# RWKV time mixing on one core: a store moved behind each crossbar transpose, three loads issued one unit later

## The chip, the core and the metric

The kernel runs on one core of a Trainium2 chip. The metric is the device time of one execution in microseconds (us), lower being better; before the change three runs have a median of 201.7 us (201.13 to 202.95). The core has a matrix engine (TensorE, "PE" in the profile, with its weight loads as "PEld"), a vector engine (DVE), a scalar engine (ACT), a general engine (POOL, also GpSimd), and a sync engine (SP) that here only issues transfers. Transfers run on 16 DMA engines that all issuers share.

## What is computed

For x of 16 batches by 2048 positions by 256 channels, in float32:

```python
x_prev[:, 1:, :] = x[:, :-1, :]           # zero at the first position
xv = x * time_mix_v + x_prev * (1 - time_mix_v)
xr = x * time_mix_r + x_prev * (1 - time_mix_r)
v = xv.reshape(-1, d_model) @ value_weight
r = xr.reshape(-1, d_model) @ receptance_weight
r_sigmoid = 1.0 / (1.0 + np.exp(-r))
out = (r_sigmoid * v).reshape(-1, d_model) @ output_weight
```

The key branch of the reference does not reach the output, and the kernel does not compute it.

## The kernel before

The work is cut into 64 **units** of 512 positions, four to a batch; unit g belongs to batch g // 4. For every unit TensorE makes the receptance product (into `psum_r`), ACT its sigmoid (`s_sb`, L591), TensorE the value product (`psum_v`), DVE the product of both (`z_sb`, L639), and, one or two units later, TensorE the output product (`psum_o`), which ACT copies into an output tile (L405). The mixing with the shifted input is made on DVE, POOL and ACT (`mix`: a scaled copy, L306, L316 or L571, and an addition, L328). POOL does one scaled copy per unit, after the additions that DVE makes for that unit.

All of it needs x with channels on the partitions. There are two ways to that:

- Batches 0 to 9 are loaded into SBUF as bf16, transposed by TensorE (`ps_t`, L250) and copied out by ACT (L267).
- Batches 10 to 15 are loaded and cast by POOL's DMA queue into a DRAM tile (`x_both`, L148, or in two halves, L144, for batches 12 and 15), and a **crossbar transpose** issued from SP (L231, `by_dma`) brings three batches at a time into SBUF (`xt_both`). The first, for batches 10 to 12, is issued in unit 27, the second, for 13 to 15, in unit 39 (`T_AT`). Each waits for the landing of all its loads.

The order on every engine is the order of the program; nothing is rescheduled. So SP issues stores and transposes one after another, and one that waits holds up all behind it. POOL's scaled copies and the loads that POOL issues stand in one queue as well.

The outputs of two units, a pair, share one tile of 1 MB (`o_sb`, or in the later part four tiles of the `x_bf` pool) and go out with one store when the second unit of the pair has been copied. What is done with the store of a pair is decided in `output` by the number of that second unit, g:

```python
            if g in FIRST:
                firsts.setdefault(FIRST[g], []).append(pair)
            elif g in WAITING:
                kept.setdefault(WAITING[g], []).append(pair)
            else:
                store(nc.sync, *pair)
```

A store under `FIRST` is issued in the unit given there, in front of the transpose, after the first half of the last load of the group has landed (`after=half`). A store under `WAITING` is issued in that unit, behind the transpose. All others are issued at once. `STAGE_AT` names the units in which POOL issues the loads of batches 13, 14 and 15, at the end of the unit, behind POOL's scaled copy; each of these loads also waits for the landing of the first crossbar transpose (`last_t`).

Of the kernel before, what the change touches and what calls it, by code (L numbers as in the profile page):

```python
# [15 lines left out]
def kernel(  # L16
# [42 lines left out]
    FREE = CROSS  # L59
    LATE_O = CROSS - 2  # L60
    T_AT = {27: 10, 39: 13}
    FIRST = {25: 27, 29: 39}
    WAITING = {31: 39, 33: 39, 35: 39}
    STAGE_AT = {34: 13, 35: 14, 36: 15}
    GROUPS = [(2, 3), (4, 5, 6), (7, 8, 9), (10, 11, 12), (13, 14, 15)]
    HALVED = (12, 15)
    SPARE = 9 * UB // 2
# [60 lines left out]
    def load(b):  # L128
        if b >= STAGED:
            group = next(q for q in GROUPS if b in q)  # L130
            if b == group[0]:
                x_both[b] = dpool.tile([len(group), P, J, D], BF16, name="x_both")
            x_bf[b] = x_both[group[0]][b - group[0]]
        else:
            x_bf[b] = xpool.tile([P, J, D], BF16, name="x_bf")
        if b < BYUNIT:
            for e in range(UB):
                nc.gpsimd.dma_start(
                    out=x_bf[b][:, e * UJ : (e + 1) * UJ, :], in_=unit_rows(x, b, e)[:, 0]
                )  # L140
            return
        if b in HALVED:
            return [
                nc.gpsimd.dma_start(out=x_bf[b][:, j : j + J // 2], in_=rows(b)[:, j : j + J // 2])  # L144
                for j in (0, J // 2)
            ]
        run = 8192 if b < LONG else 16384
        return nc.gpsimd.dma_start(out=x_bf[b], in_=rows(b), max_dma_last_dim=run)  # L148
# [165 lines left out]
    def scale_pool(piece, after):  # L314
        b, m, _, _ = piece
        op = nc.gpsimd.tensor_scalar(  # L316
            out=mixed(piece)[:, :, 1],
            in0=xt[b][:, slots(piece), 1],
            scalar1=c_sb[:, m, 1:2],
            scalar2=1.0,  # L320
            op0=ALU.mult,
            op1=ALU.mult,
        )
        tc.add_manual_dep(op.ins, after.ins.name, SYNC, reason="one at a time")
# [67 lines left out]
    def output(g, z):  # L392
# [20 lines left out]
        elif e % 2 == 1:  # L413
            pair = (b, (e - 1) * UJ, (e + 1) * UJ)
# [5 lines that stand above are left out]
# [159 lines left out]
    for g in range(NU - 1):  # L579
# [65 lines left out]
        for p in pooled[g]:  # L645
            wrap_slots(p, after=last)
            scale_pool(p, last)
        if g in STAGE_AT:
            b = STAGE_AT[g]
            loads[b] = load(b)  # L650
# [40 lines left out]
```

## Time and profile before

| | |
|---|---|
| median of three runs | 201.7 us |
| profiled execution: time, span | 202.56 us, 200.8 us |
| granted TensorE clock | 0.997 |
| 1 MB stores from `o_sb`, from `x_bf` | 24 and 4 |
| first crossbar transpose: issued, landed | 104.50 us, 120.23 us |
| loads of batches 13, 14, 15 issued | 120.76, 122.44, 124.16 and 124.72 us |
| second crossbar transpose issued | 139.90 us |
| last store issued, landed | 196.38 us, 199.62 us |

Instruction times in the profile are counted from the start of the span. A busy share is an average over the whole run; the share of the DMA engines in a stage says whether transfers queue there, and the time from the issue of a transfer to its landing says how long that queue is. A wait is put down to the event that came last before it ended as far as the semaphores tell; where the engine named had been done long before, the real releaser was another, often a DMA. In the same way the time in which SP writes out a transpose (13.69 and 13.03 us) is listed as if it were a wait. The window sums give, for a stretch of the span, each engine's busy time with the number of instructions, then the granted clock, the share of the DMA engines' time, and what they moved. That share can read somewhat over 1 in the transposes, where packets overlap.

Sigmoids of ACT (L591) mark the units: unit 27 begins at 93.75 us, unit 34 at 114.17, unit 35 at 117.05, unit 36 at 119.42, unit 39 at 128.08, unit 50 at 157.87 and unit 62 at 190.17.

### The profile page before, as it was taken

What the parts mean: (1) busy time and instruction counts of PE and PEld (TensorE: products, weight loads), DVE (VectorE), ACT (ScalarE), POOL (GpSimd) and SP (SyncE); (2) the same over time, 40 slices, a digit from 0 to 9 for tenths busy, and PEclk for the clock granted to TensorE, in tenths of its full rate; (3) what the DMA queues carried; (4) which work ended last, traced back from release to release, by engine and by line L of the source; (5) the groups of instructions that cost most, each with busy time, mean ns of one, the idle gap of its engine ahead of it and who ended that gap; (6) DMA issues with size and microseconds to landing.
All of it is one profiled execution on the core that took longest, in us unless ns stands there. A gap on an engine that the chain in (4) does not pass through costs nothing.

```text
span 200.8 us, 3819 instructions
## 1 busy us (share of the span) xinstructions
PE 192.8 (96%) x1389; PEld 122.7 (61%) x1389; DVE 184.6 (92%) x289; ACT 179.2 (89%) x209; POOL 84.1 (42%) x115
## 2 busy tenths in 40 slices
PE   8999999999999999999999999899999899999990
PEld 7556676666666666666666665466666456666670
DVE  0999999999999999899999997999999999999970
ACT  3699899999999999999999999889999899999980
POOL 1765543363542446342442329444444434444200
PEclk9999999999999999999999999999999999999998
DMA  5999999999999999999988999999999999999994
GB/s 177 219 186 217 222 282 273 277 283 273 295 308 292 297 274 286 286 281 309 313 339 175 212 324 237 212 207 297 180 239 330 418 433 423 418 415 416 402 361 176
DMA packets 36555, 58.05 MB, mean 289 GB/s; under 512 B 25781, under 2 KB 27065, under 8 KB 32697
## 3 DMA queue, kind: packets, MB, share of 16 engines
q1 hardware_dynamic: 32176, 41.29, 59.6%
q0 software_dynamic: 4208, 16.39, 41.3%
q8 instruction: 11, 0.18, 0.3%
q10 hardware_dynamic: 152, 0.13, 0.2%
q14 instruction: 8, 0.06, 0.1%
HBM read 34.34 MB, written 39.85 MB: 369 GB/s over the span
## 4 chain that ended last, share of the span: by engine, by line
PE 67%; DMA 21%; ACT 4%; POOL 3%; issue 2%; DVE 1%; SPq 0%; POOLq 0%; DVEq 0%
PE psum_v L336 20%; PE psum_o L360 19%; PE psum_r L336 18%; DMA xt_both<-x_both 16%; PE ps_t L250 7%; DMA x_bf<-in_x_dram 2%; DMA w_f<-n_receptance_weight_dram 2%; POOL mix L316 2%; ACT xt_both L267 1%; PE ps_t L360 1%; ACT o_sb L405 1%; ACT s_sb L591 1%; DVE z_sb L639 1%; ACT mix L571 1%; POOL x_both L148 1%
## 5 line engine op out<-in xcount | busy, mean ns | idle before, releaser
L316 POOL TENSOR_SCALAR mix<-xt_both,c_sb 128x1024 bf16<-128x1024 bf16 (+1 forms) x55 | 61.3, 1114 | 87.2 <-DVE mix L328 83.8
L328 DVE TENSOR_TENSOR mix<-mix,xt_both 128x1024 bf16<-128x1024 bf16 x112 | 77.5, 702 | 2.4 <-POOL mix L316 1.0
L639 DVE TENSOR_TENSOR z_sb<-s_sb,psum_v 128x1024 bf16<-128x1024 bf16 (+1 forms) x64 | 76.7, 1200 | 3.0 <-PE psum_v L336 1.3
L336 PEld LDWEIGHTS <-w_bf 128*128 128x128 bf16 x516 | 48.8, 98 | 40.4 <-issue 1.2
L591 ACT ACTIVATE s_sb<-psum_r 128x1024 bf16<-128x1024 f32 x63 | 65.1, 1034 | 5.2 <-PE psum_r L336 4.9
L336 PE MATMUL psum_v<-mix,w_bf 128*128 128x512 bf16 (+1 forms) x256 | 65.3, 377 | 0.9 <-DVE z_sb L639 0.8
L336 PE MATMUL psum_r<-mix,w_bf 128*128 128x512 bf16 (+1 forms) x252 | 64.3, 377 | 0.0
L360 PE MATMUL psum_o<-wo_bf,z_sb 128*128 128x256 bf16 x486 | 63.2, 272 | 0.7 <-ACT o_sb L405 0.7
L360 PEld LDWEIGHTS <-z_sb 128*128 128x128 bf16 x512 | 49.7, 98 | 20.6 <-issue 2.0
L405 ACT COPY o_sb<-psum_o 128x1024 f32<-128x1024 f32 x50 | 51.1, 1022 | 5.1 <-PE psum_o L360 5.1
L267 ACT COPY xt_both<-ps_t 128x1024 bf16<-128x1024 bf16 x32 | 32.8, 1034 | 0.0
L250 PEld LDWEIGHTS <-x_bf 128*128 128x128 bf16 x304 | 19.6, 98 | 9.0 <-DMA x_bf<-in_x_dram 1.9
L250 PE MATMUL ps_t<-ident,x_bf 128*128 128x128 bf16 x304 | 22.7, 219 | 0.2
L306 DVE TENSOR_SCALAR mix<-xt_both,c_sb 128x1024 bf16<-128x1024 bf16 (+1 forms) x47 | 21.1, 458 | 0.0
L571 ACT ACTIVATE mix<-xt_both,c_sb 128x1024 bf16<-128x1024 bf16 x14 | 16.2, 1158 | 0.0
L328 DVE TENSOR_TENSOR mix<-mix,xt_first 128x1024 bf16<-128x1024 bf16 x15 | 10.7, 717 | 0.1
L405 ACT COPY x_bf<-psum_o 128x1024 f32<-128x1024 f32 x10 | 10.1, 1014 | 0.0
L306 DVE TENSOR_SCALAR mix<-xt_first,c_sb 128x512 bf16<-128x512 bf16 x22 | 6.5, 348 | 0.3 <-ACT xt_first L260 0.2
L267 ACT COPY xt_first<-ps_t 128x1024 bf16<-128x1024 bf16 x6 | 6.2, 1026 | 0.0
L148 POOL DMA_DIRECT2D x_bf<-in_x_dram x8 | 5.7, 714 | 0.0
L491 POOL COPY xt_first<-xt_first 128x254 bf16<-128x254 bf16 x5 | 2.0, 395 | 6.6 <-DVE mix L328 6.6
L316 POOL TENSOR_SCALAR mix<-xt_first,c_sb 128x512 bf16<-128x512 bf16 x6 | 4.1, 689 | 0.7 <-DVE mix L328 0.2
(70 smaller groups left out, 55.6 us busy)
## 6 DMA issues: line engine op xcount, KB each, us to landing
out_dram<-o_sb SPq DMA_DIRECT2D x24, 1024.0 KB, 15.0
x_bf<-in_x_dram POOLq DMA_DIRECT2D x8, 1024.0 KB, 21.1
x_both<-in_x_dram POOLq DMA_DIRECT2D x4, 1024.0 KB, 13.8
out_dram<-x_bf SPq DMA_DIRECT2D x4, 1024.0 KB, 12.4
x_both<-in_x_dram POOLq DMA_DIRECT2D x4, 512.0 KB, 17.8
x_bf<-in_x_dram POOLq DMA_DIRECT2D x6, 256.0 KB, 6.2
out_dram<-x_bf SPq DMA_DIRECT2D x6, 256.0 KB, 4.4
o_sb<-in_x_dram SPq DMA_DIRECT2D x4, 256.0 KB, 3.8
```

Source lines behind the costliest of these rows:

```text
L148: return nc.gpsimd.dma_start(out=x_bf[b], in_=rows(b), max_dma_last_dim=run)
L250: nc.tensor.transpose(out=ps[:, jj], in_=src[:, jj, ko * P : (ko + 1) * P], identity=idn)
L267: nc.scalar.copy(out=xt[b][:, j0 : j0 + UJ], in_=ps)
L306: nc.vector.tensor_scalar(out=mixed(piece)[:, :, ko], in0=xt[b][:, slots(piece), ko], scalar1=c_sb[:, m, ko : ko + 1], scalar2=None, op0=A ...
L316: op = nc.gpsimd.tensor_scalar(out=mixed(piece)[:, :, 1], in0=xt[b][:, slots(piece), 1], scalar1=c_sb[:, m, 1:2], scalar2=1.0, op0=ALU.mul ...
L328: return nc.vector.tensor_tensor(out=mixed(piece), in0=mixed(piece), in1=xt[b][:, slots(piece, 1)], op=ALU.add)
L336: nc.tensor.matmul(out=ps[:, mo, :], lhsT=w_bf[:, m, ko, mo * P : (mo + 1) * P], rhs=mixed((b, m, e * TU + lo, e * TU + hi))[:, :, ko], st ...
L360: nc.tensor.matmul(out=ps[:, slot, :], lhsT=z[:, ko, jj * P : (jj + 1) * P], rhs=wo_bf[:, ko, :], start=(ko == 0), stop=(ko == KO - 1),)
L405: nc.scalar.copy(out=o[:, j0 : j0 + UJ, :], in_=ps)
L571: nc.scalar.activation(out=mixed(piece)[:, :, ko], in_=xt[b][:, slots(piece), ko], func=ACT.Copy, scale=c_sb[:, m, ko : ko + 1],)
L591: nc.scalar.activation(out=s_sb, in_=ps_r, func=ACT.Sigmoid)
L639: nc.vector.tensor_tensor(out=z_sb[:, :, c : c + n], in0=s_sb[:, :, c : c + n], in1=ps_v[:, :, c : c + n], op=ALU.mult,)
```

## The change

Three tables of unit numbers are altered, nothing else:

```diff
     T_AT = {27: 10, 39: 13}
-    FIRST = {25: 27, 29: 39}
-    WAITING = {31: 39, 33: 39, 35: 39}
-    STAGE_AT = {34: 13, 35: 14, 36: 15}
+    FIRST = {23: 27, 27: 39}
+    WAITING = {25: 27, 29: 39, 31: 39, 33: 39, 35: 39}
+    STAGE_AT = {35: 13, 36: 14, 37: 15}
```

The stores keep their order among each other. On SP's queue both transposes move one place ahead:

```text
before: ... 21  23  25*  [10-12]  27  29*  [13-15]  31  33  35  37 ...
after:  ... 21  23*  [10-12]  25  27*  [13-15]  29  31  33  35  37 ...
        numbers: second unit of the pair stored; * waits for a half load; [ ] crossbar transpose
```

The store of units 22 and 23, issued at once before, now waits for the first half of batch 12; the store of units 24 and 25 goes behind the first transpose; the store of units 26 and 27 takes the place between the halves of batch 15; the store of units 28 and 29 goes behind the second transpose. On POOL's queue the loads of 13, 14 and 15 each move behind one more scaled copy. The instructions of PE, DVE and ACT and their order are the same.

## The prediction

> A difference under 1% (about 2 us) can hardly be told from none here: the three runs before lie between 201.13 and 202.95 us. "Store 23" below is the 1 MB store of the pair of units 22 and 23, named by its second unit; T10 and T13 are the two crossbar transposes, named by their first batch.
>
> **What bounds the kernel now.** I read first the page's busy shares and slices.
>
> ```profile
> PE 192.8 (96%) x1389; PEld 122.7 (61%) x1389; DVE 184.6 (92%) x289; ACT 179.2 (89%) x209; POOL 84.1 (42%) x115
> ...
> DMA  5999999999999999999988999999999999999994
> GB/s 177 219 186 217 222 282 273 277 283 273 295 308 292 297 274 286 286 281 309 313 339 175 212 324 237 212 207 297 180 239 330 418 433 423 418 415 416 402 361 176
> ```
>
> TensorE is nearly full, but so are the DMA engines, and the last eight slices run at 400 to 430 GB/s: stores alone, at their peak. So two things can set the end. Next, the chain of waits round the two transposes:
>
> ```profile
> 104.50 15.73 DMA xt_both<-x_both
> 120.27 0.47 issue
> 120.76 0.57 POOL x_both L148
> 121.36 1.13 POOL mix L316
> 122.49 0.50 POOL x_both L148
> 123.02 1.18 POOL mix L316
> 124.20 0.81 POOL x_both L144 x2
> 125.27 1.14 POOL mix L316
> 126.43 1.17 ACT mix L571
> ...
> 139.90 16.64 DMA xt_both<-x_both
> 156.77 1.01 ACT o_sb L405
> ```
>
> T10 lands at 120.2; only then may POOL issue the load of batch 13, and POOL's multiplications queue behind it. T13 starts when the last half of batch 15 has landed (139.8), and the chain runs through it to ACT. The waits of 114 to 131 us give what the first costs:
>
> ```profile
> POOL x_both L148 <- DVE mix L328: 3.2, 1, 3.2
> ...
> DVE mix L328 <- POOL mix L316: 1.0, 1, 1.0
> PE psum_v L336 <- DVE z_sb L639: 0.8, 2, 0.6
> ```
>
> POOL stands 3.2 us (DVE is named there, but was done; it ended with T10's landing), DVE then 1.0, TensorE 0.8. The sigmoids of units 38 and 40 start 6.45 us apart where two units elsewhere in this stage take 5.2: this stall is 1.24 us. The second, at T13, is 0.75 us of ACT waiting for its landing (0.73 of TensorE); the work before it was ready at 155.8, T13 landed at about 156.5. Last, the stages (columns: window, busy time of PE, PEld, DVE, ACT, POOL, clock, DMA share, GB/s):
>
> ```profile
> 104.00:106.00 2.00, 2.00 (x19) 1.44 (x18) 1.88 (x4) 1.80 (x3) 1.12 (x1) 1.00 0.34 141
> 122.00:138.00 16.00, 15.16 (x93) 8.82 (x92) 14.98 (x21) 14.43 (x19) 8.94 (x13) 1.00 1.01 196
> 156.00:190.00 34.00, 33.27 (x207) 19.94 (x205) 33.40 (x45) 32.00 (x39) 13.46 (x12) 1.00 1.01 419
> 195.00:198.00 3.00, 0.80 (x5) 0.23 (x4) 0.77 (x3) 0.87 (x3) 0.00 (x0) 1.00 0.89 321
> ```
>
> The loads of 13 to 15 fill the DMA by themselves (share 1.01 from 122 to 138). From 156 to 195 stores fill it: those issued at 156.65, 157.96 and 159.25 take 11.85, 12.98 and 14.12 us to land, so 2.43 us apart (1.05 MB in 2.43 us is 431 GB/s), and the one of 161.82 takes 17.5. That queue empties only at about 195, as TensorE ends: from 195 to 198 the DMA is idle 0.11 x 3 = 0.33 us. **So TensorE and the store queue end together**, both counted from T13.
>
> **What the skill says.** "DMA: Bandwidth & Descriptors", section "Issuing engines are not separate DMA queues": transfers of all issuers share the same 16 engines. The trace agrees: from 84 to 104 the two queues take 52.1% and 50.3%. The same page, "Anatomy of one DMA", says that DMA engines wait for no semaphore, the issuing sequencer does. The trace agrees: SP stands up to 18.5 us at L372 for a load, with all later stores behind it. "Advanced Engine Details and Errata", section "X-Bar Transpose (TRN2)", calls transposes as fast as other DMAs; here 3.15 MB in 15.73 us are 200 GB/s against 431 for stores, and I use the trace.
>
> **The change part by part.** No instruction of PE, DVE or ACT is added, removed or moved; bytes stay.
>
> 1. SP's order. The stores keep their order; both transposes come one store earlier. Ahead of T10, store 25 is gone and store 23 takes its wait for the first half of batch 12; store 25 is issued behind T10. Likewise store 27 is now the one between the halves of batch 15, and store 29 goes behind T13.
>  Store 23 waits from 87.8 to 99.3, where that half landed. Behind it on SP stand T10, which needs the second half anyway, and stores 25 and 27. Their tiles: seven o_sb tiles rotate, so store 23's is written again by unit 44 (copied some 147 us in) and store 29's by unit 50 (about 164), while it should land at about 158. That 6 us cover is the shortest; without it each us late would be an ACT stall of up to 1 us. I cost it at nothing.
> 2. T10 starts earlier. At 99.3 the DMA held the rest of the half (some 0.28 MB by the packets of the load queue), store 23 and store 25. Without store 25, and with store 23's packets only starting some 1.4 us after its issue, the half should land between 101 and 103, so T10 starts 1.5 to 3.5 us sooner, by 2.4 in the middle (one store's 2.43), and lands at about 117.8 (116.8 to 118.7). Bounds: 0 (the half's tail waits on slow engines, not on store 25) and 3.5.
> 3. Loads 13 to 15 come one unit later. At unit 35 the multiplication's input is ready at 118.65 (end of the two L328 of 117.35); with no wait ahead POOL does it from 118.74 to 119.86 (1.12 a piece) and issues load 13 at about 119.9, T10 having landed 2 us before. That is 0.9 us before the 120.76 of now, though a unit later in the program. Loads 14 and 15 follow at about 122.6 and 125.1 to 125.7 (now 122.44 and 124.16 to 124.72); each load takes some 5.8 us of a full DMA ((139.5 - 122.2)/3), so a later issue of these is hidden by load 13 and 14 in flight. If that cover were gone, it would cost 1.0 us, the distance of 124.72 and 125.7. The POOL issues (0.57, 0.55, 1.09 us) lie in gaps of 1.6 us between its multiplications.
>  So load 15 lands, and T13 starts, 0.9 us earlier: 139.0. Up to 1.35, as load 13 no longer shares its first 0.45 us with a store (store 27 landed at 122.65); down to 0 if T10 stays where it was.
> 4. TensorE. Stall 1 (1.24 us) goes. What is late next is T13: work reaches it 1.24 us sooner, T13 lands 0.9 sooner, so stall 2 grows by 0.34, and TensorE ends 0.9 us earlier (0 to 1.24).
> 5. The last stretch. Behind T13 there is one store more: 2.43 us of a full DMA. It starts 0.9 earlier and takes up the idle 0.33. End: +2.43 - 0.9 - 0.33 = **+1.2 us**; with the 0.45 half counted, **+1.0**. As each store waits for the eighth before it and 17.5/2.43 = 7 are out now, SP may stand a little more; the DMA stays full, so nothing is added.
>
> The profiled execution took 202.56 us (span 200.8), 0.86 over the median; it gives 203.6, and against the median of 201.7 **202.7 us**. The bounds of step 3 (0 to 1.35 with 2.43 - 0.33) give +0.7 to +2.1; if the tail hides more idle time than 0.33 (its rate falls from 431 to some 360 GB/s), up to 0.5 goes off: +0.2 to +2.1.
>
> **Rivals.**
> - Faster, TensorE sets the end: if the store queue is empty before the last units, the extra store is hidden and only step 4 counts: -0.9, at most -1.24, 200.5 to 200.8 us. For it: 96% TensorE, the fall of GB/s to 361 in the last slice but one. Against it: the 17.5 us and the full 190 to 195.
> - Slower, the loads are bound by issue: if a later load 15 means a later landing, T13 starts 1.0 us later instead of earlier; stall 2 grows by 1.24 + 1.0, and the queue ends at 1.0 + 2.43 - 0.33 = +3.1 us, 204.8. It decides once the DMA has a gap between loads 13, 14 and 15. Against it: share 1.01 and transfers longer than the issue distance. For it: T10's earlier end leaves the DMA idle until load 13, so that time is already given away.
> - Nothing: T10's gain passes whole into T13's start (2.4) and pays for the store moved: 0, 201.7 us. POOL's place at 119.9 speaks against it.
>
> **How the numbers follow.** Forecast 0.58, faster rival 0.14, slower rival 0.17, nothing 0.11. Over +2.0 us lie all of the slower rival and 0.07 of the forecast: 0.24. Below -2.0 lies next to nothing of any, only a misread of the store queue or a shorter transpose: 0.05. Within: 0.71. The range from 200.9 to 204.3 leaves out the half of the slower rival and the tail of the faster.
>
> **What would show it.** T10 starting at about 102; a DMA gap between store 25 and load 13; load 13 at about 120 with no POOL wait; no TensorE stall at 124 to 129; T13 at about 139; a longer stall at 156; stores of 160 to 190 with latencies some 2 us longer, and the last landings some 5 us after TensorE's end instead of 4. The forecast is wrong if T13 starts at or after 139.9, or if the stores of 190 and later land as fast as now.

## The result, and the profile after

| | before | after |
|---|---|---|
| median of 20 runs | 201.52 us | 203.42 us |
| ratio, with its 95% interval | | 1.009 (1.0071 to 1.0108) |
| profiled execution: time, span | 202.56, 200.8 us | 202.64, 200.9 us |
| first transpose issued, landed | 104.50, 120.23 us | 100.91, 116.72 us |
| load 13 issued; last half of 15 landed | 120.76; 139.77 us | 119.55; 137.58 us |
| second transpose issued | 139.90 us | 137.72 us |
| last output copied; last store landed | 196.26; 199.62 us | 193.87; 199.69 us |

The changed kernel is slower by 0.9%, 1.8 us. The two profiled executions hide that: 202.56 lies 1.0 us above its median, 202.64 lies 0.8 below. The ratios leave out runs more than 1.5% above the fastest of their kernel; these were ten of e3's 22 below (203.4 to 205.0 us; median of all 22 202.06) and four of e2's 22 (203.5 to 205.3), against none of the 67 of before taken beside them, so the ratios of e3 and e2 speak of their other executions, and what made the long ones stays open.

Part 4 of the page, the shares of the chain of waits by engine, for the kernel before and for the changed one, and then the end of the chain of the changed one (start, length, what):

```profile
PE 67%; DMA 21%; ACT 4%; POOL 3%; issue 2%; DVE 1%; SPq 0%; POOLq 0%; DVEq 0%
```

```profile
PE 87%; DVE 4%; DMA 2%; SPq 1%; POOL 1%; issue 1%; DVEq 0%; POOLq 0%
```

```profile
192.69 0.73 PE ps_t L360 x4
193.42 0.02 issue
193.45 0.42 DVE x_bf L382
```

Before, the transposes held 16% of the chain; now none. The two stalls of TensorE are gone: the waits of 114 to 131 us have neither the load in front of POOL nor any matmul:

```profile
POOL mix L316 <- DVE mix L328: 9.0, 7, 2.3
ACT s_sb L591 <- PE psum_r L336: 1.1, 3, 0.4
PEld L360 <- issue: 0.2, 1, 0.2
```

By these two views the kernel got better: the last output is copied at 193.87 us, 2.4 us sooner. But the chain ends there and the span ends at 200.9. What lies between is no computation, and only the stores show it. From part 6 of the pages, of before and then of the changed kernel (queue, count, size, median us from issue to landing):

```profile
out_dram<-x_bf SPq DMA_DIRECT2D x4, 1024.0 KB, 12.4
...
out_dram<-x_bf SPq DMA_DIRECT2D x6, 256.0 KB, 4.4
```

```profile
out_dram<-x_bf SPq DMA_DIRECT2D x4, 1024.0 KB, 13.7
...
out_dram<-x_bf SPq DMA_DIRECT2D x6, 256.0 KB, 6.4
```

The last store is issued at 196.58, 2.7 us after its data was there, and lands 5.8 us after that data; before, it was issued 0.12 us after its data and landed 3.4 us after it. SP does not wait for data there: from 189.7 us on it issues store after store without a pause, and one issue keeps it 0.7 to 1.2 us, where 0.33 us was enough at 183.7 and 186.5 us. What makes an issue longer at the end is not shown. The window sums (busy times, clock, DMA share, GB/s) of before, and then of the changed kernel, show where the DMA lost time and where it had none to spare:

```profile
118.00:120.00 2.00, 2.00 (x15) 1.22 (x14) 2.00 (x4) 1.55 (x3) 0.00 (x0) 1.00 1.26 316
120.00:122.00 2.00, 2.00 (x13) 1.03 (x11) 2.00 (x4) 2.00 (x3) 1.21 (x2) 1.00 1.07 455
```

```profile
118.00:120.00 2.00, 2.00 (x15) 1.30 (x14) 2.00 (x3) 1.55 (x2) 1.52 (x2) 1.00 0.31 131
120.00:122.00 2.00, 2.00 (x13) 1.13 (x12) 2.00 (x4) 2.00 (x4) 0.87 (x2) 1.00 0.77 123
...
190.00:195.00 5.00, 3.41 (x28) 2.18 (x25) 2.68 (x6) 2.83 (x7) 0.00 (x0) 1.00 1.02 388
195.00:198.00 3.00, 0.00 (x0) 0.00 (x0) 0.00 (x0) 0.00 (x0) 0.00 (x0) 1.00 0.93 341
```

Between store 25 (landed at 119.14) and the packets of load 13 the DMA stands idle for about 0.69 x 2 + 0.23 x 2 = 1.84 us by these shares. Before there is no such hole. At the end it is nearly full to 198 while every engine has finished.

### The profile page after: what moved, and what is told of

The parts are those of the page before. It is cut to its first block, busy times and chain, and to the rows that moved or that the text cites. A ratio compares the mean times of both kernels' runs of the same rounds, so it can differ in the third digit from the quotient of the medians.

```text
span 200.9 us, 3818 instructions
## 1 busy us (share of the span) xinstructions
PE 191.8 (96%) x1389; PEld 122.8 (61%) x1389; DVE 184.0 (92%) x289; ACT 179.3 (89%) x209; POOL 84.0 (42%) x115
## 4 chain that ended last, share of the span: by engine, by line
PE 87%; DVE 4%; DMA 2%; SPq 1%; POOL 1%; issue 1%; DVEq 0%; POOLq 0%
PE psum_v L336 26%; PE psum_o L360 26%; PE psum_r L336 26%; PE ps_t L250 7%; DMA w_f<-in_value_weight_dram 2%; DVE mix L328 1%; PE ps_t L360 1%; DVE mix L306 1%; DVE z_sb L639 1%; SPq L160 1%; PE ps_t L336 0%; POOL x_bf L148 0%; POOL mix L316 0%; DVE w_bf L527 0%; SPq L166 0%
```

## The experiments

**The store-queue theory:** the end is the issue of the second transpose plus the queue of stores behind it, and the store moved behind it makes that queue longer. Below, the **first move** is the one at the first transpose (store 25 goes behind it, store 23 takes its place), the **second move** the one at the second transpose (store 29 goes behind it, store 27 takes its place). **Rivals:** the later loads are the cost; or the earlier first transpose is; or the end hangs on TensorE's last unit.

### e7, e8, e10, e11: both kernels again

Nothing edited; one execution each. With the two profiled executions above they make three **takes** of each kernel.

> The kernel before once more, for its spread from run to run. Store-queue theory: stall of TensorE at load 13 of 1.2 us, second transpose issued at 139 to 140, the last store issued as soon as its data is copied and landed some 3.2 us later.

> The changed kernel once more. Store-queue theory: no stall at load 13, second transpose issued at 137.5 to 138.5, TensorE done 1 to 2.4 us earlier than before, but the last store issued 2 us or more after its data is there, and landed 5 us or more after it. Rival (TensorE's end sets the time): its last store lands 3.2 us after its data.

> The kernel before a third time. Store-queue theory: second transpose issued between 137.4 and 139.9 us; last landing within 0.4 us of the later of two times: that issue + 59.6, and the last output's copy + 3.2.

> The changed kernel a third time. Store-queue theory: second transpose issued between 137.7 and 138.5, last landing 62.0 us (within 0.2) after that issue, 1.5 us or more later than the last output's copy + 3.2.

| us | time | first transpose issued | second issued | last output copied | last landing | landing less second issue |
|---|---|---|---|---|---|---|
| before | 202.56 | 104.50 | 139.90 | 196.26 | 199.62 | 59.7 |
| e7, before | 200.78 | 102.38 | 137.43 | 194.68 | 197.82 | 60.4 |
| e10, before | 201.15 | 102.92 | 138.17 | 195.44 | 198.19 | 60.0 |
| after | 202.64 | 100.91 | 137.72 | 193.87 | 199.69 | 62.0 |
| e8, after | 203.23 | 101.98 | 138.33 | 194.61 | 200.27 | 61.9 |
| e11, after | 203.57 | 101.69 | 138.63 | 194.84 | 200.53 | 61.9 |

In the changed kernel the end follows the second transpose to within 0.1 us (61.9 to 62.0), and comes 5.7 to 5.8 us after the last copy. In e7 and e10 it comes 3.1 and 2.8 us after the last copy: there the store queue does not set it. Small misses: e7's second transpose came 1.6 us sooner than the 139 expected, e11's 0.1 us later than 138.5, and e10 ended 0.45 us sooner than the later of its two times. TensorE's delay at load 13, as the prediction measured it (by the sigmoids: those of units 35 and 40 start 14.0, 13.3 and 14.0 us apart in the three takes of before, and 12.8 us in those of after), was 1.2, 0.5 and 1.2 us, so e7 fell short of the 1.2 expected for it. The windows of e10, and then of e11, show the difference in the last stretch:

```profile
190.00:195.00 5.00, 4.98 (x41) 3.57 (x39) 3.52 (x7) 4.06 (x9) 0.00 (x0) 1.00 0.85 322
195.00:198.00 3.00, 0.00 (x0) 0.00 (x0) 0.42 (x1) 0.06 (x1) 0.00 (x0) 1.00 0.77 274
```

```profile
190.00:195.00 5.00, 4.37 (x37) 3.03 (x34) 3.64 (x7) 3.74 (x8) 0.00 (x0) 1.00 1.03 397
195.00:198.00 3.00, 0.00 (x0) 0.00 (x0) 0.00 (x0) 0.00 (x0) 0.00 (x0) 0.98 1.00 367
```

In the usual execution of before the DMA already has room from 190 on (share 0.85; 0.81 in e7). The execution that I predicted from was the one of three in which it was full there; its first transpose came 1.6 to 2.1 us later than in the others.

### e4 and e5: one store less, in each kernel

```diff
+            if g == 33:
+                return
             if g in FIRST:
```

> The changed kernel without the store of units 32 and 33, which stands behind the second transpose (these 1 MB of the output are left unwritten). Store-queue theory: 2.43 us less, 201.0 us, ratio to before 0.9975; floor 2.6 us less, where the last unit's own store sets the end. Rival (the end is TensorE's last unit and the fixed time of its store): no change against the changed kernel, 203.4 us, ratio 1.009.

> The kernel before without the store of units 32 and 33 (left unwritten). Store-queue theory with TensorE and the queue ending together: at most 0.6 us less, 200.9 to 201.5 us, ratio 0.997 to 1.0, since TensorE's last store then sets the end. Rival (before is bound by the queue alone): 2.4 us less, 199.1 us, ratio 0.988.

e4: 201.28 us, ratio to before 0.9976 (0.9954 to 0.9997), that is 2.1 to 2.3 us less than the changed kernel. e5: ratio 0.9999 (0.9973 to 1.0025), no change. So the same store costs nearly its whole 2.43 us in the changed kernel and nothing in the one before. In e4's trace the last store lands 3.1 us after its data, as it does in e7. This is the plainest evidence for the queue: the rival that TensorE's last unit sets the end holds for the kernel before, and not for the changed one. The six stores of 256 KB in e5's page take 4.1 us to land (after: 6.4):

```profile
out_dram<-x_bf SPq DMA_DIRECT2D x6, 256.0 KB, 4.1
```

### e2 and e1: the loads alone

e2 is the kernel before, e1 the changed kernel, each with the other's loads:

```diff
 e2, against before
-    STAGE_AT = {34: 13, 35: 14, 36: 15}
+    STAGE_AT = {35: 13, 36: 14, 37: 15}
 e1, against after
-    STAGE_AT = {35: 13, 36: 14, 37: 15}
+    STAGE_AT = {34: 13, 35: 14, 36: 15}
```

> The kernel before with only the loads of 13 to 15 issued a unit later. Store-queue theory (the end is the landing of the second transpose plus the stores queued behind it): the first transpose still lands near 120.2 us, load 13 follows at about 120.3, the second transpose starts at 139.6 to 140.2 as before; the TensorE stall at 124 to 129 us is gone and the one at the second transpose grows to about 2 us; end as before, 201.5 us, ratio to before 0.997 to 1.003. Rival (the later loads are the whole cost): 203.4 us, ratio 1.009.

> The changed kernel with the loads of 13 to 15 put back to units 34 to 36. Store-queue theory: the first transpose lands at about 116.7, load 13 is issued at about 117.3 (behind the scaled copy of unit 34) and fills the 2 us in which the DMA stood idle before it; the second transpose starts some 2.0 us earlier than in the changed kernel, about 135.7, and the queue ends as much earlier: 201.4 us, ratio to before 0.996 to 1.002. Rival (an idle DMA there costs nothing, the end hangs on something after the second transpose): 203.4 us, ratio 1.009.

e2: 201.65 us, ratio 0.9996 (0.9969 to 1.0023); only its times are read here, so what was expected of its stalls stays open. e1: 202.07 us, ratio 1.0009 (0.9982 to 1.0035). The later loads alone leave the median where it was (201.65 beside 201.59); in the changed kernel, putting them back takes nearly all of the loss away. The reason that the traces of before, after and e1 suggest is that load 13 finds different things in front of it. In the kernel before, the transpose lands so late (118.2 to 120.2) that load 13, ready on POOL, waits for it; it is issued 0.53 us after that landing in all three takes, and the store behind the transpose covers the time until its packets flow. In the profiled execution of the changed kernel both are over at 119.1, and a load issued at 119.6 leaves a hole; in its three takes the hole is 1.8, 1.3 and 1.9 us by the same sums. In e1, with load 13 issued at 117.82, there is none:

```profile
118.00:120.00 2.00, 2.00 (x14) 1.19 (x13) 2.00 (x4) 1.55 (x3) 1.45 (x2) 1.00 0.98 320
120.00:122.00 2.00, 2.00 (x13) 1.03 (x11) 2.00 (x4) 2.00 (x3) 0.87 (x3) 1.00 1.27 197
```

The second transpose of e1 was issued at 137.30, 0.4 to 1.3 us sooner than in the takes of after, not the 2.0 expected. Probably a load in flight while store 25 is still being moved only shares the DMA with it: load 13 takes 8.1 us to land there and 7.5 in the profiled execution of after. The end of e1 is 62.0 us after that issue, as in the changed kernel, since as many stores stand behind.

### e3, e6 and e9: the stores, one move at a time

e3 keeps the changed kernel's first move and loads but puts the second transpose's stores back; e6 is e3 with the loads in units 34 to 36; e9 is the kernel before with the second move alone.

```diff
 e3 and e6, against after
-    FIRST = {23: 27, 27: 39}
-    WAITING = {25: 27, 29: 39, 31: 39, 33: 39, 35: 39}
+    FIRST = {23: 27, 29: 39}
+    WAITING = {25: 27, 31: 39, 33: 39, 35: 39}
 e9, against before
-    FIRST = {25: 27, 29: 39}
-    WAITING = {31: 39, 33: 39, 35: 39}
+    FIRST = {25: 27, 27: 39}
+    WAITING = {29: 39, 31: 39, 33: 39, 35: 39}
```

> The changed kernel with the second transpose's stores put back: only the store of units 24 and 25 goes behind the first transpose (loads a unit later). Store-queue theory: first transpose at about 101 us, stores 25 and 27 fill the gap before load 13, second transpose at about 138.2, one store fewer behind it than in the changed kernel: 1.5 us below before, 200.0 us, ratio 0.993. Rival (later loads are the cost): 203.4 us, ratio 1.009. Rival (an early first transpose costs by itself): slower than before too.

> As e3 (only the store of units 24 and 25 behind the first transpose) with the loads put back to units 34 to 36. Here two stores follow the first transpose and already fill the DMA until load 13, so the store-queue theory says no difference to e3 (0.9973, 0.994 to 1.000): the second transpose starts at the same 138. Rival (later loads cost by themselves): 1 to 2 us below e3, ratio 0.988 to 0.992.

> The kernel before with only the second transpose's stores changed (27 between the halves of batch 15, 29 behind the transpose), loads in units 34 to 36 as before. Store-queue theory: no store follows the first transpose, so the DMA stands idle for 1 to 2 us until the packets of load 13, which start no sooner than before; the second transpose is issued at 138 to 139.5, its end is 62.0 us after that (one store more than before's 59.5): 1.5 to 2.4 us slower than before, 203.1 to 204.0, ratio 1.007 to 1.012. Rival (the earlier first transpose or the later loads are what costs): as before, ratio 0.998 to 1.002.

e3: ratio 0.9973 (0.9946 to 1.0000). e6: 201.18 us, 0.9991 (0.9971 to 1.0011). e9: 203.12 us, 1.0066 (1.004 to 1.0092).

So **the loss needs the second move, and the first alone costs nothing**. Without the second move no combination is slower by its ratio (e2, e6 and e3); with the second alone it is 1.0066, with both moves 1.0009, with both and the later loads 1.009. The second move with the later loads and without the first was not run. e9, where first transpose and loads are handled as before, is 1.3 us slower (0.0066 x 201.6), a little less than expected. Its second transpose is issued at 138.46 and it ends 62.0 us later, at 200.48, like the three takes of after and e1. And it has the hole, because no store follows its first transpose:

```profile
118.00:120.00 2.00, 2.00 (x13) 1.02 (x12) 2.00 (x4) 1.71 (x2) 0.26 (x1) 1.00 0.72 161
120.00:122.00 2.00, 1.86 (x13) 1.04 (x11) 2.00 (x2) 1.83 (x3) 1.82 (x3) 1.00 0.46 66
```

0.28 x 2 + 0.54 x 2 = 1.64 us. Its second transpose comes no sooner than in the takes of before (138.50 on average), although one store less is moved ahead of the loads: the hole takes that time.

With the first move alone the earlier first transpose is harmless (e6), which refutes that rival. Stores 25 and 27 then both stand behind it, and in e3 some 0.9 us of the hole are left (shares of 1.09 and 0.56 from 118 to 122). e3 was expected at 0.993, and its interval ends at 0.9946: the gain was over-estimated. In its trace the second transpose is issued at 138.19, as expected, but the last output is copied at 194.07 and the last store lands 3.3 us later, at 197.35: TensorE's end sets it, and a shorter queue no longer helps. That e6 and e3 agree within their intervals, and that e6 is not at 0.988 to 0.992, fits later loads that cost nothing where the DMA has work, as far as e3's ratio goes.

No version was clearly faster than before: the gain of e3 (0.3%) reaches 1.0 with its interval.

## Why the prediction came out as it did

The forecast of slower by about half a percent, 202.7 us, had the right mechanism and too small a size (measured 203.42).

- **The order on SP, and the cover of the tiles:** held. In no trace of the changed kernel does a copy of ACT wait for a store.
- **The first transpose at about 102:** held: 100.91, 101.98 and 101.69, landing at 116.7 to 118.2.
- **Load 13 at about 119.9, with no wait on POOL and a gap of the DMA before it:** held: 119.55, 120.11, 120.27. The idle DMA was named as the slower rival's support, and it is where the gain of the earlier first transpose is lost: over three takes each the first transpose landed 1.7 us sooner (117.4 for 119.1), and the second was issued hardly sooner.
- **The second transpose 0.9 us earlier:** the profiled pair gives 2.2, but that is the spread of before. Over three takes each it is 138.50 before and 138.23 after, 0.3 us.
- **TensorE:** the delay at load 13 went, as said. A longer stall at the second transpose, the next thing to be late, did not come (0.00, 0.06 and 0.12 us); it had been worked out from an execution whose transpose was unusually late. TensorE ended earlier, by 1.0 us over the takes (last output copied at 194.4 for 195.5; forecast 0.9), and that bought nothing.
- **The last stretch, and where the size was lost.** The forecast let the time from the second transpose to the end grow by 2.43 - 0.33 = 2.10 us. Over three takes each it grew by 1.9 (60.0 to 61.9), so this term was nearly right; the slack that the extra store fills is 0.5 us rather than 0.33, since in the usual execution of before the queue does not set the end. What was too large is what was taken off for the earlier second transpose: 0.9 us, and half of 0.45 more, where the takes show 0.3. 1.9 less 0.3 is 1.6 us, about the difference between the means of the three takes (203.15 and 201.50); the medians of 20 runs lie 1.9 apart, which three takes each do not resolve.
- **TensorE and the store queue end together:** so it was in the profiled execution alone. e5, e7 and e10 show that TensorE usually ends last before the change. The forecast took one execution for the kernel, and that this cost it only 0.2 us of slack is partly luck. A small misreading stands beside it: the slices of 400 to 430 GB/s are seven (402 to 433), with 361 and 176 behind them, not the last eight.
- **The rivals:** the faster one (TensorE sets the end) is right about the kernel before, as e5 shows, and wrong about the changed one, as e4 shows. The slower one has the second transpose start 1.0 us later than before; it starts no later (138.2 for 138.5), and e2 is no slower. But it was right that the lateness of the loads matters: in the changed kernel they are what makes the loss, 1.009 with them and 1.0009 without (e1). The third, that the earlier first transpose pays for the store, holds only with the earlier loads: it is e1, at 1.0009.

What stays open is why the first transpose of the kernel before starts anywhere between 102.4 and 104.5 us; no run here took that apart.

## What to carry to other kernels

A store moved past a long transfer doesn't vanish: it is free only if something else fills its old place or the queue at the end has room, and otherwise the DMA idles there and the same bytes stand in the queue at the end. Find out what ends last in several executions, as two limits that meet in one profile may lie apart in the next (here by up to 0.7 us, e7's 60.4 less 59.7). And read past the chain of waits: here it got shorter by 2.4 us and free of stalls while the kernel became slower, and only the time from issue to landing of the last stores told.

## What the runs showed of the hardware

The time told is the last landing plus 2.9 to 3.0 us in all six takes of both kernels (200.78 less 197.82 is 2.96; 203.57 less 200.53 is 3.04), so the last landing is the event to work towards. A crossbar transpose of 3 MB does not have a fixed length: the first one took from 15.1 us (e4) to 16.6 us (e9) from issue to landing. An issue of a store does not have one either: it kept SP 0.33 us where stores stood far apart and up to 1.2 us at the end of the changed kernel, where the queue was full.
